# Whole-matrix Strassen products of a decoder layer: block sums on VectorE, additions by accumulating transfers

## The chip, the core and the metric

The kernel runs on one core of a Trainium2 chip. A core has a matmul engine (TensorE, here PE, with its weight load PEld), VectorE (DVE), ScalarE (ACT) and GpSimd (POOL), and SyncE (SP), which here issues all transfers. PE writes to PSUM, in banks of 128 x 512 fp32 numbers; the other operands lie in SBUF, 128 partitions wide. The metric is the device time of one execution in microseconds (us), median of the runs.

## The reference

One layer of a decoder trunk with x of 1024 tokens by 1024 features, fp32. Cut to what matters here:

```python
h  = rmsnorm(x)                      # three token mixers of h: A, B, C
m  = gate_a * A + gate_b * B + gate_c * C
x1 = x + m @ w_out                   # [1024,1024] @ [1024,1024]
h2 = rmsnorm(x1)
act = conv3(h2 @ w_up) * gelu(h2 @ w_gate)   # width 2816, schematic
x2 = x1 + act @ w_down               # [1024,2816] @ [2816,1024]
out = rmsnorm(x2)
```

## The kernel before

Activations lie feature-major, in tiles of 128 features by 1024 tokens. Each fp32 operand of a matmul is split into a high part (a cast on ACT, L96) and a low part (a subtraction, mostly on DVE, L97), and a product is made of three passes of a 128x128 weight against 512 columns. Instructions are put in order by a scheduler from the program's text; each engine then runs its own list in that order.

The end of the attention merges the three branches: `merge_c` makes the third branch's product tile by tile, DVE multiplies the bank by its gate (gc, L1131), and POOL adds the result onto the sum of the other two (ga, L1132). The second half of the tokens is done first. yc is the operand of these products.

`strassen_full` (L720) multiplies a whole matrix by Strassen's scheme in Winograd's form: weights and activations are cut into 2 x 2 blocks, there are seven products instead of eight, and their operands are sums of blocks. It is called for w_out (4 slices of the inner dimension) and for w_down (11 slices). Its items are (p, j): product p in the order 0, 1, 2, 3, 5, 4 and slice j. An item has 12 matmuls (4 output tiles by 3 passes), one of p = 2 has 24, since it stands for two products. For each item, one after the other and a little ahead of the matmuls: `loads` has SP fetch the weight blocks (fr) and activations (act), `sums` makes the block sums in place (S1 L785, T3 L786 and S2 L787 on POOL, T2 L788 and T1 L789 on DVE, all for p = 2; S3 L793, T4' L796 and S4 L800 on POOL for p = 3, 4 and 5), and `splits` makes fw (weights) and ft (activations). When a product has ended, `after(p)` says what is done with its PSUM banks: ACT copies a bank to a tile (cc, L834), SP loads the residual block x and an engine adds the copy (`add_x`, L824 and L825), later products are added from PSUM (`plus`, L829). What is put off by `later` is spread over the next items, three pieces at each.

A finished block goes to `done`. For w_out that is `done1`: the block's operands for the FFN (hb, T1 to T4), its store, and its square, which POOL adds to a running sum ssb, one sum for each half of the tokens (L952); a matmul of ssb with ones (L134), a root on ACT and a few steps on DVE (L119 to L127) give 1/rms (rs), which a matmul with ident (L142) spreads over the partitions. While the last sums come, PE makes F0, the first FFN weight tile's products, 96 matmuls with hb. For w_down `done2` squares by `add_sq` (L160), with the addition on DVE (L168). The FFN between the two, about 821 to 1234 us of the span, is made by pairs of weight tiles and is not touched.

Of the kernel before, what the change touches and what calls it, by code (L numbers as in the profile page):

```python
# [18 lines left out]
P = 128  # L19
# [10 lines left out]
# columns of the small packed constants  # L30
# [9 lines left out]
# columns of the wide packed constants  # L40
# [7 lines left out]
def trunk_kernel(  # L48
# [65 lines left out]
    def rsqrt(a, n, act=True):  # L114
        """a ** -0.5 on a positive [P, n] tile: an estimate (from a square root, or halved exponent bits), then
        Newton's steps."""
        y, t = tiny(n, "rs0", 2), tiny(n, "rs1", 2)
        if act:
            nc.scalar.activation(out=t, in_=a, func=AF.Sqrt)  # L119
            nc.vector.reciprocal(out=y, in_=t)  # L120
        else:
            nc.vector.tensor_scalar(out=y.bitcast(I32), in0=a.bitcast(I32), scalar1=-0.5, scalar2=float(0x5f3759df),
                                    op0=ALU.mult, op1=ALU.add)
        for _ in range(1 if act else 3):
            nc.vector.scalar_tensor_tensor(out=t, in0=y, scalar=-0.5, in1=y, op0=ALU.mult, op1=ALU.mult)
# [11 lines left out]
    def bcast_rows(rs, nt, dst, pool):  # L137
        """dst[:, t*128 + n] = rs[n, t] on all partitions."""
# [21 lines left out]
    def add_sq(acc, blk, alloc):  # L160
        """acc + blk ** 2, acc None at first."""
# [15 lines left out]
    def op2(src, alloc, n="op"):  # L177
        """two operands from a [P, 1024] tile."""
# [12 lines left out]
    # [feature, token] operands of a normalised activation, block by block  # L191
    class Act:
# [5 lines left out]
        def winograd(self, xt, j, T4=True, eng=None):  # L198
            """the block sums of slice j, made in place."""
# [15 lines left out]
        def block(self, kt, j):  # L215
            """name the operand of a block."""
# [3 lines left out]
    def prepare(src):  # L220
        """operands of a pair of weight tiles."""
# [25 lines left out]
    def strassen_pair(src, h, alloc_ps, mid=lambda: None):  # L247
        """both [128, 1024] products of a pair of weight tiles."""
# [59 lines left out]
    def scaled(kt, j):  # L308
        """operands of x times the gain; the token's factor follows the product."""
# [10 lines left out]
    def squares(kt, j):  # L320
        """sums of squares, in two parts."""
# [38 lines left out]
    # keeps the tensor engine's clock up until the first operands are there  # L360
# [15 lines left out]
    def rel_bias():  # L376
        """relative-position bias, one value per distance, replicated over 128 rows in DRAM."""
# [97 lines left out]
    # lambda of the differential attention, on all partitions  # L475
# [8 lines left out]
    # DRAM scratch  # L484
# [7 lines left out]
    # values of the attention, token-major  # L492
# [33 lines left out]
    def pooling(zb):  # L526
        """means over the trailing windows minus the value, feature-major."""
# [22 lines left out]
    def gating(f):  # L550
        """spatial gating (two groups at once; the diagonal blocks are kept)."""
# [42 lines left out]
    # q, k feature-major, stored as hi / lo  # L594
# [21 lines left out]
    def load_head(hd):  # L616
        """steps of the loads of a head."""
# [30 lines left out]
    def scores(t, c):  # L648
        """one map's exponentials of a query tile (the scores are negated)."""
# [40 lines left out]
    # the bias of zeros ties the table's load to the last gate  # L690
# [8 lines left out]
    def first_tiles():  # L699
        """the loads of the first head and its first scores."""  # L700
# [19 lines left out]
    def strassen_full(src, w, nsl, x_d, out, done, tail=None, LL=4):  # L720
        """steps of out[d][:, half] = (w.T @ src)[d tile] + x_d; w: [2*nsl, P, 1024], src(k): fp32 tile k, spent in
        place. done(d, half): what follows each block; tail(operands) takes over the last NL slices.
        The first LL steps only prepare."""
        pool, vec, sub, add = nc.gpsimd, nc.vector, ALU.subtract, ALU.add
        LS, LP = 2, 2
        SE = (nc.gpsimd, nc.gpsimd, nc.gpsimd, nc.vector, nc.vector, nc.gpsimd, nc.gpsimd, nc.gpsimd)
# [15 lines left out]
        def wh(p, k, lo_, c):  # L742
            """column half c of weight tile lo_ + k, two tiles at a time."""
# [36 lines left out]
        def sums(p, j):  # L780
            b11, b12, b21, b22 = blocks(j) if p > 1 else [None] * 4
            if p == 2:
                r, q, k = T[p, j]
                t1 = c2("T1")
                SE[0].tensor_tensor(out=q, in0=r[:, NH:], in1=q, op=add)          # S1  # L785
                SE[1].tensor_tensor(out=b12, in0=b22, in1=b12, op=sub)            # T3  # L786
                SE[2].tensor_tensor(out=k, in0=q, in1=r[:, :NH], op=sub)          # S2  # L787
                SE[3].tensor_tensor(out=b11, in0=b12, in1=b11, op=add)            # T2  # L788
                SE[4].tensor_tensor(out=t1, in0=b22, in1=b11, op=sub)             # T1  # L789
                T[p, j] = (k, b11), (q, t1)  # L790
            if p == 3:
                r = T[p, j]
                SE[5].tensor_tensor(out=r[:, :NH], in0=r[:, :NH], in1=r[:, NH:], op=sub)  # S3  # L793
                T[p, j] = (r[:, :NH], b12),
            if p == 4:
                SE[6].tensor_tensor(out=b21, in0=b21, in1=b11, op=sub)            # T4'  # L796
                T[p, j] = (T[p, j], b21),
            if p == 5:
                r = T[p, j]
                SE[7].tensor_tensor(out=r, in0=r, in1=keep(j), op=sub)            # S4  # L800
# [13 lines left out]
        B, X, C = {}, {}, {}  # L814
# [12 lines left out]
        def plus(d, j, other, eng):  # L827
            t = out(d, j)
            eng.tensor_tensor(out=t, in0=t, in1=other, op=ALU.add)  # L829

        def copy(key, d):
            if d % 2 == 0:
                C[key, d // 2] = a4([P, 2, NH], n="cc")
            nc.scalar.copy(C[key, d // 2][:, d % 2, :], B[0][d])  # L834

        def cc(key, d):
            return C[key, d // 2][:, d % 2, :]
# [5 lines left out]
        def after(p):  # L843
            R4 = range(4)
            if p == 0:
                for d in R4:
                    later(1, copy, 0, d)
                    later(1, lambda d: add_x(d, 0, cc(0, d), pool), d)
            if p == 1:
                for d in R4:  # L850
                    plus(d, 0, B[1][d], vec)
                for d in R4:
                    fin(d, 0, 3)
            if p == 2:
                for d in R4:
                    copy(2, d)
                for d in R4:
                    later(3, lambda d: add_x(4 + d, 1, B[2][d], vec), d)
                    later(4, lambda d: add_x(d, 1, cc(2, d), pool), d)
            if p == 3:  # L860
                for d in R4:
                    copy(3, d)
                for d in R4:
                    later(4, lambda d: plus(4 + d, 1, cc(3, d), pool), d)
                    fin(4 + d, 1, 5)
                for d in R4:
                    later(4, lambda d: add_x(4 + d, 0, cc(3, d), pool), d)
            if p == 5:
                for d in R4:
                    plus(d, 1, B[2][d], vec)  # L870
                    fin(d, 1, 5)
            if p == 4:
                for d in R4:
                    plus(4 + d, 0, B[4][d], vec)
# [6 lines left out]
        for n in range(-LL, len(items)):  # L881
            for st_ in stages:
                # operands of the held slices are made ahead
# [4 lines left out]
            if n >= 0:  # L888
# [18 lines left out]
                if p == 4 and tail:  # L907
                    if j == nsl - NL - 1:
                        for d in range(4):
                            plus(4 + d, 0, B[4][d], vec)  # L910
# [17 lines left out]
    def op_g(src, g, n):  # L928
        """operand of src times a gain."""
# [6 lines left out]
    def done1(d, j):  # L936
# [8 lines left out]
        def square():  # L945
# [22 lines left out]
        def t2():  # L968
            # T3 first: it needs the raw block
# [32 lines left out]
    def combine(t):  # L1002
        """rows scaled by sum0: P0 - (lam * sum0 / sum1) * P1."""
# [10 lines left out]
    def transpose(t, g):  # L1014
        """four key blocks of a query tile."""
# [13 lines left out]
    def attend(t):  # L1029
        """steps of the product with the values; tokens on the partitions."""  # L1030
# [16 lines left out]
    def sub_norm(hd, js, pool):  # L1047
        """rms norm over the head's channels; the rows carry the factor sum0."""
# [74 lines left out]
    def merge_c(banks):  # L1123
        for n_, (j, m) in enumerate((j, m) for j in (1, 0) for m in range(KT)):
# [7 lines left out]
            nc.gpsimd.tensor_tensor(out=mg[m][:, half(j)], in0=mg[m][:, half(j)], in1=gc, op=ALU.add)  # L1132
# [108 lines left out]
    # FFN down, final norm  # L1241
# [16 lines left out]
    def scale_out(k, j, sl, r, eng):  # L1258
        """two output blocks."""
# [28 lines left out]
    def tail2(hold):  # L1288
        """the last blocks, a quarter of the tokens at a time."""
# [94 lines left out]
def _layout(i):  # L1384
    """Layouts of the inputs, and constants of the shapes alone."""
# [10 lines left out]
    def pairs(wa, wb):  # L1396
        """[pair, (first, second), p, 8 * 128]: the second's K halves are swapped."""
# [65 lines left out]
```

## Time and profile before

| what | value |
|---|---|
| three runs | 1494.07, 1494.66, 1498.56 us; median 1494.66 |
| span of the profiled execution | 1492.7 us |
| busy PE, DVE, ACT, POOL | 1373.6, 1091.0, 649.0, 827.3 us |
| w_out (first matmul on ft, fw) to the first FFN pair | 671 to 821 us |
| w_down, without the tail | about 1235 to 1465 us |

The span is that of one execution under the profiler, without what lies around it, and is 2.0 us below the median of the runs. "PE busy" is no proof of PE at its peak: at full rate its matmuls overlap, so the number of matmuls that start in a window is the better measure. An arrow in a row points from the waiting engine to the one whose result it waited for.

### The profile page before, as it was taken

What the parts mean: (1) busy time and instruction counts of PE and PEld (TensorE: products, weight loads), DVE (VectorE), ACT (ScalarE), POOL (GpSimd) and SP (SyncE); (2) the same over time, 40 slices, a digit from 0 to 9 for tenths busy, and PEclk for the clock granted to TensorE, in tenths of its full rate; (3) what the DMA queues carried; (4) which work ended last, traced back from release to release, by engine and by line L of the source; (5) the groups of instructions that cost most, each with busy time, mean ns of one, the idle gap of its engine ahead of it and who ended that gap; (6) DMA issues with size and microseconds to landing.
All of it is one profiled execution on the core that took longest, in us unless ns stands there. A gap on an engine that the chain in (4) does not pass through costs nothing. (4 is left out here: it accounts for less than half of the span.)

```text
span 1492.7 us, 17887 instructions
## 1 busy us (share of the span) xinstructions
PE 1373.6 (92%) x6502; PEld 1137.8 (76%) x6502; DVE 1091.0 (73%) x1402; ACT 649.0 (43%) x1057; POOL 827.3 (55%) x499
## 2 busy tenths in 40 slices
PE   7899999999998989897875999999999999689887
PEld 6698778888886877786654888888888888478776
DVE  8764766444446899887899566877778789896783
ACT  7342234344445666523454434333333344154551
POOL 6423366555545454367597455666666624956724
PEclk9899999999999999998998999999999999899998
DMA  5232154333349954434521122222222268335413
GB/s 179 91 114 93 44 189 148 113 113 113 114 126 279 258 157 141 149 119 132 192 85 57 57 71 92 78 85 85 85 85 85 85 218 316 128 97 178 163 64 113
DMA packets 72496, 189.97 MB, mean 127 GB/s; under 512 B 7566, under 2 KB 16910, under 8 KB 72408
## 3 DMA queue, kind: packets, MB, share of 16 engines
q1 hardware_dynamic: 72408, 188.83, 38.2%
q8 instruction: 51, 0.84, 0.2%
q14 instruction: 37, 0.30, 0.1%
HBM read 143.70 MB, written 47.46 MB: 128 GB/s over the span
## 5 line engine op out<-in xcount | busy, mean ns | idle before, releaser
L185 PE MATMUL b<-ft,fw 128*128 128x512 f32 (+1 forms) x1308 | 307.2, 394 | 43.4 <-DVE fw L97 16.6
L185 PEld LDWEIGHTS b<-ft,fw 128*128 128x128 f32 x1308 | 245.8, 194 | 102.2 <-DVE fw L97 19.0
L347 POOL TENSOR_TENSOR F<-F,RB 128x1024 f32<-128x1024 f32 x74 | 190.5, 2575 | 164.6 <-DVE F L256 145.7
L256 DVE TENSOR_TENSOR F<-b,c 128x512 f32<-128x512 f32 x152 | 100.8, 683 | 125.8 <-ACT c L275 71.5
L185 PE MATMUL b<-hb,Ah 128*128 128x512 f32 x608 | 191.5, 395 | 0.0
L97 DVE TENSOR_TENSOR Sl<-s,Sh 128x1024 fp32r<-128x1024 f32 x76 | 150.8, 1985 | 42.6 <-PE b L185 23.5
L228 POOL TENSOR_TENSOR s<-r 128x512 f32<-128x512 f32 x38 | 60.8, 1599 | 194.5 <-DMA r<-in_w_up 77.4
L185 PE MATMUL b<-T,Sh 128*128 128x512 f32 x504 | 154.3, 389 | 0.0
L185 PEld LDWEIGHTS b<-hb,Ah 128*128 128x128 f32 x608 | 115.2, 190 | 25.1 <-issue 1.0
L185 PE MATMUL b<-hb,Al 128*128 128x512 f32 x304 | 119.5, 393 | 0.8 <-DVE Al L97 0.8
L96 ACT CAST Sh<-s 128x1024 fp32r<-128x1024 f32 x76 | 80.0, 1053 | 89.0 <-DVE Al L97 51.9
L97 DVE TENSOR_TENSOR Al<-r,Ah 128x1024 fp32r<-128x1024 f32 x38 | 77.5, 2038 | 50.8 <-ACT Ah L96 36.1
L185 PEld LDWEIGHTS b<-T,Sh 128*128 128x128 f32 x504 | 94.6, 188 | 19.8
L97 DVE TENSOR_TENSOR fw<-fr,fw 128x512 fp32r<-128x512 f32 x90 | 86.5, 976 | 19.7 <-ACT fw L96 18.6
L185 PE MATMUL b<-T,Sl 128*128 128x512 f32 x252 | 96.9, 389 | 0.0
L185 PE MATMUL b<-hb,Sh 128*128 128x512 f32 x304 | 94.1, 391 | 1.4 <-DVE F L256 1.4
L96 ACT CAST fw<-fr 128x512 fp32r<-128x512 f32 x90 | 54.3, 621 | 80.4 <-DVE fw L97 31.1
L96 ACT CAST Ah<-r 128x1024 fp32r<-128x1024 f32 x38 | 40.0, 1052 | 100.9 <-PE b L185 97.4
L185 PE MATMUL b<-Tl,Sh 128*128 128x512 f32 x204 | 79.4, 389 | 0.0
L185 PE MATMUL b<-Th,Sh 128*128 128x512 f32 x204 | 78.7, 390 | 0.7 <-ACT c L266 0.7
L185 PE MATMUL b<-Th,Sl 128*128 128x512 f32 x204 | 78.5, 389 | 0.0
L97 DVE TENSOR_TENSOR ft<-act,ft 128x512 fp32r<-128x512 f32 x66 | 73.5, 1141 | 4.8 <-ACT ft L96 4.8
(259 smaller groups left out, 3170.5 us busy)
## 6 DMA issues: line engine op xcount, KB each, us to landing
fr<-in_w_down SPq DMA_DIRECT2D x47, 512.0 KB, 3.8
r<-in_w_up SPq DMA_DIRECT2D x42, 512.0 KB, 3.7
r<-in_w_gate SPq DMA_DIRECT2D x24, 512.0 KB, 4.1
g_d<-F SPq DMA_DIRECT2D x24, 512.0 KB, 5.0
act_d<-cv SPq DMA_DIRECT2D x22, 512.0 KB, 2.6
act<-act_d SPq DMA_DIRECT2D x22, 512.0 KB, 6.3
fr<-in_w_out SPq DMA_DIRECT2D x18, 512.0 KB, 3.8
x<-in_xT SPq DMA_DIRECT2D x32, 256.0 KB, 5.1
```

The source lines that it names most:

```text
L96: nc.scalar.copy(hi, src)
L97: (eng or nc.vector).tensor_tensor(out=lo, in0=src, in1=hi.bitcast(F32), op=ALU.subtract)
L185: nc.tensor.matmul(ps, lhsT=w[a], rhs=x[b], start=first and i == 0, stop=last and i == 2, skip_group_check=more)
L228: nc.gpsimd.tensor_tensor(out=s1[:, :NH], in0=a21, in1=a22, op=ALU.add)
L256: nc.vector.tensor_tensor(out=o, in0=ps, in1=c, op=ALU.add)
L347: (eng or nc.gpsimd).tensor_tensor(out=F, in0=F, in1=RB, op=ALU.mult)
```

## The change

All eight block sums run on DVE. A new function `accumulate` has POOL issue a transfer that adds its source onto its destination in SBUF. It takes the place of three kinds of additions: the residual (`start`: ACT copies the bank into the output tile, then x is accumulated onto it from DRAM; the SP load, the cc tiles and `add_x` go), the squares' sums (in `done1`, then on POOL, and in `add_sq`, then on DVE), and the merge's last addition (POOL). There are 32, 14, 10 and 16 of them, 72 in all, each of 128 x 512 fp32 numbers, 256 KB. Comments are taken out too, which moves line numbers.

```diff
+    def accumulate(dst, src):
+        nc.gpsimd.dma_start(out=dst, in_=src, accum_op=ALU.add)
...
     def add_sq(acc, blk, alloc):
...
-        nc.vector.tensor_tensor(out=acc, in0=acc, in1=sq, op=ALU.add)
+        accumulate(acc, sq)
...
-                SE[0].tensor_tensor(out=q, in0=r[:, NH:], in1=q, op=add)          # S1
-                SE[1].tensor_tensor(out=b12, in0=b22, in1=b12, op=sub)            # T3
-                SE[2].tensor_tensor(out=k, in0=q, in1=r[:, :NH], op=sub)          # S2
+                vec.tensor_tensor(out=q, in0=r[:, NH:], in1=q, op=add)
+                vec.tensor_tensor(out=b12, in0=b22, in1=b12, op=sub)
+                vec.tensor_tensor(out=k, in0=q, in1=r[:, :NH], op=sub)
...
-        def add_x(d, j, other, eng):
+        def start(d, j, bank):
             t = out(d, j)
-            nc.sync.dma_start(out=t, in_=x_d[d, :, half(j)])
-            eng.tensor_tensor(out=t, in0=t, in1=other, op=ALU.add)
+            nc.scalar.copy(t, bank)
+            accumulate(t, x_d[d, :, half(j)])
...
             if p == 0:
                 for d in R4:
-                    later(1, copy, 0, d)
-                    later(1, lambda d: add_x(d, 0, cc(0, d), pool), d)
+                    later(1, start, d, 0, B[0][d])
...
             if p == 2:
                 for d in R4:
-                    copy(2, d)
+                    start(d, 1, B[0][d])
                 for d in R4:
-                    later(3, lambda d: add_x(4 + d, 1, B[2][d], vec), d)
-                    later(4, lambda d: add_x(d, 1, cc(2, d), pool), d)
+                    later(3, start, 4 + d, 1, B[2][d])
             if p == 3:
                 for d in R4:
-                    copy(3, d)
+                    start(4 + d, 0, B[0][d])
+                    later(4, plus, 4 + d, 1, B[0][d])
                 for d in R4:
-                    later(4, lambda d: plus(4 + d, 1, cc(3, d), pool), d)
                     fin(4 + d, 1, 5)
-                for d in R4:
-                    later(4, lambda d: add_x(4 + d, 0, cc(3, d), pool), d)
...
-                nc.gpsimd.tensor_tensor(out=stat[j], in0=stat[j], in1=sq, op=ALU.add)
+                accumulate(stat[j], sq)
...
-            nc.gpsimd.tensor_tensor(out=mg[m][:, half(j)], in0=mg[m][:, half(j)], in1=gc, op=ALU.add)
+            accumulate(mg[m][:, half(j)], gc)
```

The order of the instructions changes at three places. The first is POOL at the end of w_out, where the squares of both halves of the tokens are summed (two ssb, told apart by their last number) and the operands T2 and T3 are split (L97). Before:

```order
L952 TENSOR_TENSOR ssb_6482<-ssb_6482,sq_6644 128x512
L952 TENSOR_TENSOR ssb_6482<-ssb_6482,sq_6663 128x512
L952 TENSOR_TENSOR ssb_6482<-ssb_6482,sq_6707 128x512
L952 TENSOR_TENSOR ssb_6215<-ssb_6215,sq_6725 128x512
L952 TENSOR_TENSOR ssb_6482<-ssb_6482,sq_6718 128x512
L952 TENSOR_TENSOR ssb_6215<-ssb_6215,sq_6732 128x512
L97 TENSOR_TENSOR T_1373_6777<-x_555_3645,T_1373_6777 128x512
L952 TENSOR_TENSOR ssb_6215<-ssb_6215,sq_6739 128x512
L97 TENSOR_TENSOR T_1374_6786<-x_551_3641,T_1374_6786 128x512
L97 TENSOR_TENSOR T_1376_6801<-x_556_3646,T_1376_6801 128x512
L97 TENSOR_TENSOR T_1377_6804<-x_552_3642,T_1377_6804 128x512
L952 TENSOR_TENSOR ssb_6215<-ssb_6215,sq_6746 128x512
```

After:

```order
L104 DMA ssb_6494<-sq_6638 128x512
L104 DMA ssb_6209<-sq_6707 128x512
L104 DMA ssb_6494<-sq_6682 128x512
L104 DMA ssb_6209<-sq_6714 128x512
L104 DMA ssb_6494<-sq_6693 128x512
L104 DMA ssb_6209<-sq_6721 128x512
L97 TENSOR_TENSOR T_1367_6759<-x_555_3645,T_1367_6759 128x512
L97 TENSOR_TENSOR T_1368_6768<-x_551_3641,T_1368_6768 128x512
L97 TENSOR_TENSOR T_1370_6783<-x_556_3646,T_1370_6783 128x512
L97 TENSOR_TENSOR T_1371_6786<-x_552_3642,T_1371_6786 128x512
L104 DMA ssb_6494<-sq_6700 128x512
L104 DMA ssb_6209<-sq_6728 128x512
```

The additions have become transfers (DMA), the two sums take turns, and four T splits stand ahead of each sum's last addition.

The second is DVE in the merge, where it empties the banks (gc; `at`, `sc`, `mm` are PSUM tiles) and makes yc's low part. Before:

```order
L1131 TENSOR_TENSOR gc_5647<-at_5769,gc_5647 128x512
L932 SCALAR_TENSOR_TENSOR yc_5722<-ms_5717,cs,yc_5722 128x512
L1131 TENSOR_TENSOR gc_5740<-at_5784,gc_5740 128x512
L1131 TENSOR_TENSOR gc_5762<-mm_5799,gc_5762 128x512
L1131 TENSOR_TENSOR gc_5458<-mm_5814,gc_5458 128x512
L1131 TENSOR_TENSOR gc_5527<-sc_5829,gc_5527 128x512
L97 TENSOR_TENSOR fw_5978<-fr_5891,fw_5978 128x512
L1131 TENSOR_TENSOR gc_5584<-sc_5844,gc_5584 128x512
```

After:

```order
L1122 TENSOR_TENSOR gc_5647<-at_5769,gc_5647 128x512
L97 TENSOR_TENSOR fw_5956<-fr_5891,fw_5956 128x512
L789 TENSOR_TENSOR ga_3705<-ga_4558,ga_3705 128x512
L789 TENSOR_TENSOR ga_3846<-ga_4814,ga_3846 128x512
L923 SCALAR_TENSOR_TENSOR yc_5722<-ms_5717,cs,yc_5722 128x512
L1122 TENSOR_TENSOR gc_5740<-at_5784,gc_5740 128x512
L1122 TENSOR_TENSOR gc_5762<-mm_5799,gc_5762 128x512
L789 TENSOR_TENSOR ga_4066<-ga_5050,ga_4066 128x512
L1122 TENSOR_TENSOR gc_5458<-mm_5814,gc_5458 128x512
L1122 TENSOR_TENSOR gc_5527<-sc_5829,gc_5527 128x512
L97 TENSOR_TENSOR fw_5978<-fr_5891,fw_5978 128x512
L789 TENSOR_TENSOR ga_4322<-ga_5295,ga_4322 128x512
```

The sums T3 (L789, ga from ga and ga), which POOL made before, now stand among the evacuations, two of them ahead of yc's.

The third is PE in the last product of w_down, where the squares of one half of the tokens are summed over the partitions. Before, the product's banks being b_11338 to b_11341:

```order
L185 MATMUL b_11338<-ft_11311,fw_11308 128x512 x3
L185 MATMUL b_11339<-ft_11311,fw_11308 128x512 x3
L185 MATMUL b_11340<-ft_11311,fw_11308 128x512 x3
L185 MATMUL b_11341<-ft_11311,fw_11308 128x512 x3
L185 MATMUL b_11338<-ft_11317,fw_11314 128x512 x3
L185 MATMUL b_11339<-ft_11317,fw_11314 128x512
L134 MATMUL b_11408<-ones,ssb_11069 128x1 x4
L185 MATMUL b_11339<-ft_11317,fw_11314 128x512 x2
L185 MATMUL b_11340<-ft_11317,fw_11314 128x512 x3
```

After, the banks being b_11302 to b_11305:

```order
L189 MATMUL b_11302<-ft_11287,fw_11284 128x512 x3
L189 MATMUL b_11303<-ft_11287,fw_11284 128x512 x3
L189 MATMUL b_11304<-ft_11287,fw_11284 128x512 x3
L189 MATMUL b_11305<-ft_11287,fw_11284 128x512 x3
L189 MATMUL b_11302<-ft_11293,fw_11290 128x512 x3
L189 MATMUL b_11303<-ft_11293,fw_11290 128x512
L138 MATMUL b_11372<-ones,ssb_11065 128x1 x4
L189 MATMUL b_11303<-ft_11293,fw_11290 128x512 x2
L189 MATMUL b_11304<-ft_11293,fw_11290 128x512 x3
```

The matmul with ones stood behind 40 matmuls of the product, and now stands behind 64; POOL's list there has seven transfers onto ssb in a row, of which the last four belong to blocks that product 5 finishes.

## Rows read from the trace of the kernel before

**Rows 1.** Page, part 1: busy time, share, instructions of each engine.
```profile
PE 1373.6 (92%) x6502; PEld 1137.8 (76%) x6502; DVE 1091.0 (73%) x1402; ACT 649.0 (43%) x1057; POOL 827.3 (55%) x499
```

**Rows 2.** Windows: busy time and starts of each engine, clock, DMA share.
```profile
core 0: us, PE busy (x) PEld busy (x) DVE busy (x) ACT busy (x) POOL busy (x), PEclk, DMA share, GB/s
670.00:790.00 120.00, 96.73 (x393) 75.29 (x392) 104.70 (x93) 54.16 (x94) 89.96 (x57) 0.94 0.39 129
790.00:830.00 40.00, 23.96 (x101) 18.36 (x100) 32.73 (x31) 18.91 (x33) 28.56 (x17) 0.79 0.15 47
1240.00:1260.00 20.00, 20.00 (x90) 16.57 (x89) 19.30 (x22) 11.59 (x21) 10.28 (x7) 1.00 0.97 366
1260.00:1340.00 80.00, 61.98 (x251) 48.47 (x250) 73.23 (x67) 27.61 (x52) 61.59 (x38) 0.94 0.37 122
1340.00:1360.00 20.00, 20.00 (x90) 16.55 (x89) 8.98 (x13) 6.34 (x11) 8.00 (x6) 1.00 0.31 93
1380.00:1440.00 60.00, 54.34 (x229) 43.51 (x228) 49.48 (x53) 30.56 (x56) 36.85 (x23) 0.97 0.41 141
1440.00:1460.00 20.00, 15.91 (x65) 13.04 (x64) 8.93 (x18) 8.56 (x14) 0.00 (x0) 0.83 0.00 1
```

**Rows 3.** PE's waits, 671 to 821: total, times, longest (us).
```profile
PE b L142 <- DVE rs L127: 15.2, 1, 15.2
PE b L185 <- DVE x L829: 6.7, 2, 6.2
PE b L185 <- DVE ft L97: 6.3, 6, 1.9
PE b L185 <- ACT cc L834: 5.4, 1, 5.4
```

**Rows 4.** PE's waits, 1240 to 1480.
```profile
PE b L185 <- DVE fw L97: 16.6, 5, 8.2
...
PE b L134 <- DVE ssb L168: 4.1, 1, 4.1
```

**Rows 5.** Tile ga: DVE's splits, ns min/median/max, first and last start.
```profile
L97 DVE TENSOR_TENSOR ft<-ga,ft x24: 677/1751/1784, 661.7 to 771.2; 128x512 fp32r<-128x512 f32 x24
```

**Rows 6.** Timeline, two stretches: DVE alone, DVE beside POOL.
```profile
1433.22 4.29 DVE L97 TENSOR_TENSOR ft<-act,ft 128x512 fp32r<-128x512 f32 x7
...
698.45 1.70 POOL L825 TENSOR_TENSOR x<-x,cc 128x512 f32<-128x512 f32 x1
698.96 1.74 DVE L97 TENSOR_TENSOR ft<-T,ft 128x512 fp32r<-128x512 f32 x1
```

**Rows 7.** DMA view: transfers of 256 KB, median us from issue to landing.
```profile
x<-in_xT SPq DMA_DIRECT2D x32, 256.0 KB, 5.1
...
kh<-qk_d SPq DMA_DIRECT2D x16, 256.0 KB, 7.6
...
out<-x SPq DMA_DIRECT2D x8, 256.0 KB, 2.5
```

**Rows 8.** Lines: POOL's residual additions, busy us, mean ns, idle before.
```profile
L825 POOL TENSOR_TENSOR x<-x,cc 128x512 f32<-128x512 f32 x24 | 40.2, 1692 | 0.4 <-DMA x<-x_d 0.3
```

**Rows 9.** Timeline at 1271: ACT's wait for a load.
```profile
1271.04 0.62 ACT L96 CAST ft<-act 128x512 fp32r<-128x512 f32 x1 [7.04 <-DMA act<-act_d]
```

**Rows 10.** Timeline of the passage from w_out to the first FFN tile.
```profile
787.86 1.27 DVE L829 TENSOR_TENSOR x<-x,b 128x512 f32<-128x512 f32 x2
...
789.20 0.62 ACT L951 ACTIVATE sq<-x 128x512 f32<-128x512 f32 x1
...
804.08 5.08 DVE L978 SCALAR_TENSOR_TENSOR x<-x,cs 128x512 f32<-128x512 f32 x3
...
805.25 6.71 POOL L97 TENSOR_TENSOR T<-x,T 128x512 fp32r<-128x512 f32 x4
...
819.11 1.22 PE L142 MATMUL b<-ident,rs 128*128 128x128 f32 x4 [15.16 <-DVE rs L127]
```

**Rows 11.** Timeline at the merge: yc's low part, and its use.
```profile
649.86 0.75 DVE L932 SCALAR_TENSOR_TENSOR yc<-ms,cs,yc 128x512 fp32r<-128x512 f32 x1 [0.60 <-ACT yc L931]
...
655.11 0.61 PE L185 MATMUL mm<-yc,ph 128*128 128x512 f32 x2
```

More of the change, by code (lines that the diff above doesn't have):

```diff
@@ L720, in strassen_full @@
     def strassen_full(src, w, nsl, x_d, out, done, tail=None, LL=4):
-        pool, vec, sub, add = nc.gpsimd, nc.vector, ALU.subtract, ALU.add
+        vec, sub, add = nc.vector, ALU.subtract, ALU.add
         LS, LP = 2, 2
-        SE = (nc.gpsimd, nc.gpsimd, nc.gpsimd, nc.vector, nc.vector, nc.gpsimd, nc.gpsimd, nc.gpsimd)
         items = [(p, j) for p in (0, 1, 2, 3, 5, 4) for j in range(nsl)]
@@ L784, in sums @@
                 t1 = c2("T1")
-                SE[0].tensor_tensor(out=q, in0=r[:, NH:], in1=q, op=add)
-                SE[1].tensor_tensor(out=b12, in0=b22, in1=b12, op=sub)
-                SE[2].tensor_tensor(out=k, in0=q, in1=r[:, :NH], op=sub)
-                SE[3].tensor_tensor(out=b11, in0=b12, in1=b11, op=add)
-                SE[4].tensor_tensor(out=t1, in0=b22, in1=b11, op=sub)
+                vec.tensor_tensor(out=q, in0=r[:, NH:], in1=q, op=add)
+                vec.tensor_tensor(out=b12, in0=b22, in1=b12, op=sub)
+                vec.tensor_tensor(out=k, in0=q, in1=r[:, :NH], op=sub)
+                vec.tensor_tensor(out=b11, in0=b12, in1=b11, op=add)
+                vec.tensor_tensor(out=t1, in0=b22, in1=b11, op=sub)
                 T[p, j] = (k, b11), (q, t1)
@@ L792, in sums @@
                 r = T[p, j]
-                SE[5].tensor_tensor(out=r[:, :NH], in0=r[:, :NH], in1=r[:, NH:], op=sub)
+                vec.tensor_tensor(out=r[:, :NH], in0=r[:, :NH], in1=r[:, NH:], op=sub)
                 T[p, j] = (r[:, :NH], b12),
             if p == 4:
-                SE[6].tensor_tensor(out=b21, in0=b21, in1=b11, op=sub)
+                vec.tensor_tensor(out=b21, in0=b21, in1=b11, op=sub)
                 T[p, j] = (T[p, j], b21),
@@ L799, in sums @@
                 r = T[p, j]
-                SE[7].tensor_tensor(out=r, in0=r, in1=keep(j), op=sub)
+                vec.tensor_tensor(out=r, in0=r, in1=keep(j), op=sub)
                 T[p, j] = (r, b22),
@@ L812, in mm @@
                     first and j == 0, j == n - 1, more)
-        B, X, C = {}, {}, {}
+        B = {}
         bg = []
@@ L819, in later, with plus @@
             bg.append((due, f, a))
-        def add_x(d, j, other, eng):
+        def start(d, j, bank):
             t = out(d, j)
-            nc.sync.dma_start(out=t, in_=x_d[d, :, half(j)])
-            eng.tensor_tensor(out=t, in0=t, in1=other, op=ALU.add)
-        def plus(d, j, other, eng):
+            nc.scalar.copy(t, bank)
+            accumulate(t, x_d[d, :, half(j)])
+        def plus(d, j, bank):
             t = out(d, j)
[L829 to L837, printed above, removed]
+            vec.tensor_tensor(out=t, in0=t, in1=bank, op=ALU.add)
         def fin(d, j, due):
@@ L846, in after @@
                 for d in R4:
-                    later(1, copy, 0, d)
-                    later(1, lambda d: add_x(d, 0, cc(0, d), pool), d)
+                    later(1, start, d, 0, B[0][d])
             if p == 1:
                 for d in R4:
-                    plus(d, 0, B[1][d], vec)
+                    plus(d, 0, B[1][d])
                 for d in R4:
@@ L855, in after @@
                 for d in R4:
-                    copy(2, d)
+                    start(d, 1, B[0][d])
                 for d in R4:
-                    later(3, lambda d: add_x(4 + d, 1, B[2][d], vec), d)
-                    later(4, lambda d: add_x(d, 1, cc(2, d), pool), d)
+                    later(3, start, 4 + d, 1, B[2][d])
             if p == 3:
                 for d in R4:
-                    copy(3, d)
+                    start(4 + d, 0, B[0][d])
+                    later(4, plus, 4 + d, 1, B[0][d])
                 for d in R4:
-                    later(4, lambda d: plus(4 + d, 1, cc(3, d), pool), d)
                     fin(4 + d, 1, 5)
-                for d in R4:
-                    later(4, lambda d: add_x(4 + d, 0, cc(3, d), pool), d)
             if p == 5:
                 for d in R4:
-                    plus(d, 1, B[2][d], vec)
+                    plus(d, 1, B[2][d])
                     fin(d, 1, 5)
@@ L873, in after @@
                 for d in R4:
-                    plus(4 + d, 0, B[4][d], vec)
+                    plus(4 + d, 0, B[4][d])
                     fin(4 + d, 0, 6)
@@ L909, in strassen_full @@
                         for d in range(4):
-                            plus(4 + d, 0, B[4][d], vec)
+                            plus(4 + d, 0, B[4][d])
                 elif j == nsl - 1:
```

## The prediction

> **What bounds the kernel now.** I read the page's first part first: PE is busy for 92% of the span, DVE for 73%, POOL for 55% [rows 1]. The other 8% are some 119 us in which PE does nothing, and the question is which of them lie in the two places that the diff touches. The windows answer it [rows 2]. At full rate PE starts 90 matmuls of 512 columns in 20 us, 0.222 us each (1340 to 1360). Against that rate the whole-matrix product for w_out (670 to 790) starts 393 instead of 540 and loses 147 x 0.222 = 32.7 us; the passage from it to the first FFN tile (790 to 830) starts 101 instead of 180 and loses 17.5; the product for w_down loses 109 x 0.222 = 24.2 in 1260 to 1340, 41 x 0.222 = 9.1 in 1380 to 1440 and 25 x 0.222 = 5.6 in 1440 to 1460. Together 89 us. In the lossy windows DVE is near full (104.7 of 120, 73.2 of 80) and POOL busy too, and in 1340 to 1360, with POOL at 8 of 20, nothing is lost.
>
> The waits name the engine [rows 3, 4]: PE waits for DVE, once for 15.2 us on the root of the mean square (L127), else on splits (L97) and on PSUM additions (L829). Why DVE is late shows in its durations. The same subtraction of 128x512 with two SBUF inputs takes 677 ns at best and 1751 at the median for the operands out of the merge [rows 5]. Seven in a row, with POOL idle, go by in 4.29 us, 0.61 each from start to start; beside a POOL addition one takes 1.74, and the POOL addition 1.70 [rows 6]. So the two engines hold each other up, and the loss belongs to POOL's additions and sums in these stages.
>
> **The change part by part.** X stands below for the time from a POOL issue of an accumulating transfer of 256 KB to its landing. The trace has no transfer of POOL's. Its nearest rows are SP's transfers of the same size [rows 7]: 2.5 (a store), 5.1 (a load from the same tensor that the residuals come from), 7.6 (the slowest). Two of the slowest in a row, 15.2, is the upper bound, for a transfer that must fetch its destination as well. I take 5, the nearest row in what is read. What a page says of this stands apart: the Trainium skill, "DMA: Bandwidth & Descriptors", section "Anatomy of one DMA", has a transfer issued by GpSimd cost about 2.0 us and its bytes over 436 GB/s. By that X would be an estimated 2.6, and the sum below some 14 us lower, 1432; no run here shows it for an accumulating one.
>
> 1. POOL loses 90 block sums (S1, T3, S2, S3, T4' and S4 of 15 slices), 32 residual additions, 14 additions of squares and 16 of the merge: 152 operations at 1.69 us or a little less [rows 8], up to 257 us in which DVE's two-input operations took up to 1.74 instead of 0.68. DVE gains the 90 sums, 61 us at 0.68, and loses 10 additions of squares.
>
> 2. Is DVE then fast enough? In product 2 a slice needs 5 sums and 4 splits from DVE, 9 x 0.61 = 5.5 us, while PE's 24 matmuls take 24 x 0.222 = 5.3: a tie. In products 3 to 5 it is 3 x 0.61 = 1.8 against 2.7 for 12 matmuls, in 0 and 1 two splits. Before, product 2 gave DVE 6 operations, 10.4 us when all met POOL.
>
> 3. What w_out's 32.7 us become: the waits on x and ft (6.7 and 6.3) go. The copies of full banks stay on ACT, so I keep the whole wait on cc, 5.4 [rows 3], and 4.6 for the tie and for the lead-in. Kept 10, gained 22.7.
>
> 4. w_down, 1260 to 1340. The longest wait is 8.2 on fw, and it goes with the contention. But the loads stay, and ACT stood 7.0 us for act there [rows 9]. I keep 7 of 24.2: gained 17.2. In 1380 to 1440 I keep 5 of 9.1: gained 4.1.
>
> 5. The passage, 790 to 830. Before, PE waited 15.2 us for the root, whose DVE steps stood behind scalings of 1.7 us beside POOL's T splits [rows 10]. After, the additions of squares are a chain of transfers, each waiting for the last one, issued in POOL's order. From the end of product 4: PSUM addition and square 2.0 (787.86 to 789.82 [rows 10]), two alternating steps 2X, four T splits on POOL at 1.68 (6.7, the row of four [rows 10], since DVE is busy beside them), the last accumulate X: 8.7 + 3X = 23.7. The matmul on ssb now stands 5 before the end of F0's 96, at 91 x 0.222 = 20.2. So PE waits 3.5, then 1.5 for the root, and 1.5 goes to the clock, which the passage shows at a mean of 0.79 now [rows 2]. Kept 6.5, gained 11.0. A second floor lies close below: some 25 DVE operations from product 4's end to the root, at 0.7 each and four of them slow, are 20 to 22 us too, so a smaller X gains at most 3 here.
>
> 6. The end of w_down. Seven squares are one chain, four of them after product 5: 3 + 4X = 23 from that product's end. PE reaches its ssb matmul after 64 matmuls, 14.2 us, and waits 8.8, with 2 for the clock; before it waited 4.1 [rows 4] and the window lost 5.6. Lost 5.2 more.
>
> 7. The merge. DVE now has the T3 sums between the evacuations of gc, each behind an accumulate. The second T3 stands right before yc's low part, which DVE gave out at 649.86 before and PE used at 655.11 [rows 11]. That leaves 5.2 us of cover, about X; then two more such waits pile up before the first ft. At X = 5 I count 1.
>
> The loads of x that SP no longer issues and the tiles that the copies no longer take I cost at nothing: no wait of PE's on either is among the rows. The accumulates into x cost nothing either while X is below 10: they are issued at a product's start, and the PSUM addition onto them comes at its end, 48 matmuls or 10.7 us later.
>
> Sum: -22.7 - 17.2 - 4.1 - 11.0 + 5.2 + 1 = -48.8 us. The profiled span of 1492.7 becomes 1443.9; the median of the runs, 1494.66, lies 2.0 above the span, so 1446.
>
> **The rivals.** (a) The chain decides. Above 5, each us of X costs 3 in the passage, 4 at the end and about 2 in the merge, 9 in all; the 48.8 are used up at X = 10.4, and at 15.2 the time is 1446 + 92 = 1538. For it: the chains are serial and POOL stands still in each wait, with T splits and later issues behind it. Against it: no row of 256 KB above 7.6. At 7.6 the time is 1469. The Trainium skill, same page, "Rules for kernel authors", says that an accumulate reads its destination and writes it later and that the next access must wait for its semaphore; so nothing would let the chain overlap, and no run before shows it. Chance that it takes the whole gain or more: 0.11.
>
> (b) DVE becomes the bound in product 2. If its operations don't overlap at 0.61 but follow at their 0.68, a slice takes 6.1 against 5.3, 0.8 x 15 = 12 us: 1458. For it: a tie leaves no room for additions from PSUM between. Against it: the row of seven. Chance 0.18. (That DVE's slowness isn't POOL's doing, so that 9 operations at 1.74 make 15.7 us a slice in product 2 and 156 us more over 15 slices, would end near 1600; the paired rows [rows 6] speak against it, 0.02.)
>
> (c) The loads bound w_down: DMA share 0.97 at 1240 to 1260 [rows 2] and ACT's wait for act. Then 20 of the 24.2 stay instead of 7: 1459. Against it: the share falls to 0.37 just where the loss is. Chance 0.12.
>
> **How the numbers follow.** The forecast, 1446, has 0.57. Low end: X = 2.5 takes away the end's wait (10.8), 3 in the passage and 1 in the merge, 1431, and half of the 22 kept in steps 3 and 4 gives 1420. High end: X = 7.6 together with (b) is 1481; I take 1480. Within 0.3% (4.5 us), about what a measurement can tell, is 0.03; slower, from (a) beyond 10.4 and the remark in (b), 0.11; the rest faster, 0.86.
>
> **What would show it.** Right: POOL's rows of 1.7 gone from both stages, DVE's fw and ft near 0.69, PE at 85 or more per 20 us in 1260 to 1340, the wait for rs below 5, one of 5 to 12 on ssb near the end, X read as issue to landing near 5. Wrong: waits on ssb, ga or x that add up to 49 (a), DVE full in product 2 with PE at 80 per 20 us (b), ACT waiting for act (c).

## The result, and the profile after

| | before | after |
|---|---|---|
| median of four runs, us | 1494.37 (1493.38 to 1498.56) | 1445.78 (1444.86 to 1449.65) |
| ratio, 95% interval | | 0.9676 (0.9660 to 0.9691) |
| forecast | | 1446, range 1420 to 1480 |
| span of the profiled execution | 1492.7 | 1448.0 |

The change is faster by 48.6 us, 3.2%. The profiled execution of after is the longest of its four (1449.65), so the trace below accounts for 44.7 of these. One of the four executions of e2, below, took 2262.21 us at a granted clock of 0.555 and is left out of its numbers. The first view to read is the timeline at the places where PE passes from one stage to the next. Of after:

```profile
672.23 1.07 PE L189 MATMUL b<-ft,fw 128*128 128x512 f32 x4
...
805.34 1.20 PE L189 MATMUL b<-hb,Ah 128*128 128x512 f32 x2
...
1203.60 0.62 PE L189 MATMUL b<-ft,fw 128*128 128x512 f32 x2
...
1420.77 0.39 PE L1290 MATMUL b<-ones,ssb 128*128 128x1 f32 x3
```

and the same four starts in the trace of before:

```profile
671.20 0.62 PE L185 MATMUL b<-ft,fw 128*128 128x512 f32 x2
...
820.83 0.77 PE L185 MATMUL b<-hb,Ah 128*128 128x512 f32 x1
...
1218.83 0.39 PE L185 MATMUL b<-ft,fw 128*128 128x512 f32 x1
...
1465.60 0.28 PE L1299 MATMUL b<-ones,ssb 128*128 128x1 f32 x2
```

Their differences are the stages (w_down begins at 1218.8, earlier than the 1235 given ahead, and its last product runs on into the tail):

| stage, us | before | after | difference | forecast |
|---|---|---|---|---|
| up to w_out | 671.2 | 672.2 | +1.0 | +1 |
| w_out and the passage to the FFN | 149.6 | 133.1 | -16.5 | -33.7 |
| FFN pairs | 398.0 | 398.3 | +0.3 | 0 |
| w_down | 246.8 | 217.2 | -29.6 | -16.1 |
| tail | 27.1 | 27.2 | +0.1 | 0 |

So the sum came out and two of its parts did not: w_out gave 17 us less than forecast, w_down 13 more. The windows of after show the same. The columns are those of [rows 2]:

```profile
672.00:762.00 90.00, 80.69 (x338) 65.19 (x337) 71.09 (x96) 52.58 (x93) 33.17 (x34) 0.94 0.81 198
762.00:806.00 44.00, 27.52 (x116) 22.44 (x115) 31.48 (x41) 20.27 (x34) 22.48 (x20) 0.77 0.43 96
1215.00:1280.00 65.00, 65.00 (x289) 53.83 (x288) 64.01 (x103) 34.36 (x62) 4.41 (x5) 1.00 0.81 269
1280.00:1320.00 40.00, 36.73 (x148) 29.53 (x147) 28.68 (x48) 15.44 (x28) 1.73 (x2) 0.91 0.40 114
1320.00:1400.00 80.00, 77.83 (x342) 63.58 (x341) 60.39 (x98) 49.35 (x92) 14.01 (x16) 1.00 0.71 189
1400.00:1420.00 20.00, 20.00 (x100) 16.71 (x99) 3.69 (x10) 4.39 (x8) 2.59 (x3) 1.00 0.28 49
```

At 90 matmuls per 20 us, w_down's 1280 to 1400 lacks 50 matmuls, 11 us, where before lost 39 from 1260 to 1460 [rows 2]. From 1215 to 1280 DVE is busy for 64.0 of 65 us and PE misses nothing; PE is in products 0 and 1 there, until 1269, and DVE makes product 2's sums and splits ahead of it. The first window, w_out's 336 matmuls, lacks 67, 14.9 us. The second is the passage with F0: 96 matmuls, 21.3 us of work, in 43.2. The page's first part gives DVE 80 operations more than before and less busy time, 1013.6 us against 1091.0 [rows 1]:

```profile
PE 1364.5 (94%) x6502; PEld 1137.7 (79%) x6502; DVE 1013.6 (70%) x1482; ACT 651.7 (45%) x1065; POOL 644.4 (45%) x419
```

The groups by line, busy and mean, show why: DVE's splits take about their time alone, against the 1.75 us of [rows 5]:

```profile
L97 DVE TENSOR_TENSOR fw<-fr,fw 128x512 fp32r<-128x512 f32 x90 | 62.3, 710 | 6.6 <-ACT fw L96 5.6
L97 DVE TENSOR_TENSOR ft<-act,ft 128x512 fp32r<-128x512 f32 x66 | 44.0, 695 | 3.4 <-ACT ft L96 3.4
L97 DVE TENSOR_TENSOR ft<-ga,ft 128x512 fp32r<-128x512 f32 x24 | 16.2, 687 | 5.4 <-ACT ft L96 5.3
```

PE's waits from 600 to 820, and behind the dots from 1180 to 1440 (answers to [rows 3] and [rows 4]; the wait on ssb at the end of w_down is gone):

```profile
PE b L138 <- DMA ssb<-sq: 8.4, 1, 8.4
PE b L146 <- DVE rs L131: 8.0, 1, 8.0
PE b L189 <- DVE ft L97: 5.6, 1, 5.6
...
PE b L189 <- DVE fw L97: 3.6, 2, 2.6
```

And the transfers, in the view of [rows 7]:

```profile
ssb<-sq POOLq DMA_DIRECT2D x24, 256.0 KB, 4.2
...
ga<-gc POOLq DMA_DIRECT2D x16, 256.0 KB, 5.3
...
x<-in_xT POOLq DMA_DIRECT2D x16, 256.0 KB, 8.1
...
x<-x_d POOLq DMA_DIRECT2D x16, 256.0 KB, 8.5
```

X, taken as 5, is 4.2 and 5.3 in the median where a chain or the next reader waits for it, and 8.1 to 8.5 for the residuals, issued up to eight in a row and not on the path.

### The profile page after: what moved, and what is told of

Same layout as the page of the kernel before. It is cut to its first block, busy times and chain, and to the rows that moved or that the text cites. A ratio compares the mean times of both kernels' runs of the same rounds, so it can differ in the third digit from the quotient of the medians.

```text
span 1448.0 us, 17868 instructions
## 1 busy us (share of the span) xinstructions
PE 1364.5 (94%) x6502; PEld 1137.7 (79%) x6502; DVE 1013.6 (70%) x1482; ACT 651.7 (45%) x1065; POOL 644.4 (45%) x419
## 5 line engine op out<-in xcount | busy, mean ns | idle before, releaser
L189 PE MATMUL b<-ft,fw 128*128 128x512 f32 (+1 forms) x1308 | 298.0, 388 | 14.8 <-DVE ft L97 6.8
L189 PEld LDWEIGHTS b<-ft,fw 128*128 128x128 f32 x1308 | 243.3, 191 | 66.8 <-DVE ft L97 8.3
L97 DVE TENSOR_TENSOR Sl<-s,Sh 128x1024 fp32r<-128x1024 f32 x76 | 149.3, 1964 | 42.7 <-PE b L189 24.0
L97 DVE TENSOR_TENSOR Al<-r,Ah 128x1024 fp32r<-128x1024 f32 x38 | 77.0, 2026 | 53.1 <-ACT Ah L96 38.2
L104 POOL DMA_DIRECT2D ssb<-sq x24 | 21.1, 906 | 117.9 <-ACT sq L171 38.2
L189 PE MATMUL b<-wh,hb 128*128 128x256 f32 x384 | 71.8, 286 | 0.0
```

What stands on the lines that cost most here:

```text
L97: (eng or nc.vector).tensor_tensor(out=lo, in0=src, in1=hi.bitcast(F32), op=ALU.subtract)
L104: nc.gpsimd.dma_start(out=dst, in_=src, accum_op=ALU.add)
L189: nc.tensor.matmul(ps, lhsT=w[a], rhs=x[b], start=first and i == 0, stop=last and i == 2, skip_group_check=more)
```

## The experiments

Each is timed in rounds with the kernel before on one chip, and the ratio to it is what is compared; after has 0.9676 (0.9660 to 0.9691).

### The parts alone: the sums, the transfers

Edit of the kernel before, e1:

```diff
-        SE = (nc.gpsimd, nc.gpsimd, nc.gpsimd, nc.vector, nc.vector, nc.gpsimd, nc.gpsimd, nc.gpsimd)
+        SE = (nc.vector,) * 8
```

> The kernel before with all eight block sums on DVE; residuals, squares and the merge's addition stay where they were. If POOL's two-input operations beside DVE are what costs (contention), 90 of POOL's 152 go and most of the gain comes: 1458 to 1472 us, with DVE's fw and ft means near 0.75 us and only stretches beside the residual additions slow. If it is POOL's list that is late, with the sums as harmless fillers, DVE gets 61 us more to do and the time stays above 1485.

Edit of after, e2 (one of six lines, S1, T3, S2, S3, T4', S4):

```diff
-                vec.tensor_tensor(out=q, in0=r[:, NH:], in1=q, op=add)
+                nc.gpsimd.tensor_tensor(out=q, in0=r[:, NH:], in1=q, op=add)
```

> The changed kernel with the sums S1, T3, S2, S3, T4' and S4 back on POOL, so that the accumulating transfers stand alone. Contention: 90 POOL operations stay beside DVE's splits, the time lies at 1470 to 1482 us and DVE's splits in product 2 still show 1.7 us. If the residuals and squares on POOL's list were the delay, most of the gain stays: below 1458.

Measured: e1 1458.38 us, 0.9751 (0.9733 to 0.9770), 36.5 won; e2 1479.27 us (median of three), 0.9889 (0.9865 to 0.9912), 15.6 won. Together that is 52.2 against 48.6, by the ratios 0.0360 against 0.0324: the parts add up to the whole or, at the edge of the intervals, to a little more. In e1 the mean of DVE's splits is 839 ns (fw) and 758 (ft of act), where near 750 was expected; before it was 976 and 1141. In e2 DVE has 90 operations fewer than in after and PE still waits 11.6 us for fw from 1195 to 1475; its groups by line:

```profile
L97 DVE TENSOR_TENSOR fw<-fr,fw 128x512 fp32r<-128x512 f32 x90 | 88.1, 993 | 26.1 <-ACT fw L96 25.1
L97 DVE TENSOR_TENSOR ft<-act,ft 128x512 fp32r<-128x512 f32 x66 | 66.1, 1036 | 4.9 <-ACT ft L96 4.9
```

With less to do DVE is slower at it, 993 and 1036 ns against 710 and 695, beside POOL's sums.

These two runs don't separate two things that a sum on POOL does: it slows DVE, and it comes late itself, at 1.5 to 1.7 us each in a row on POOL's list. In w_down of before, ACT waited 30.9 us for POOL's weight sums; the largest part, six waits from 1218 to 1466, was for S2:

```profile
ACT fw L96 <- POOL S L787: 21.4, 6, 7.6
```

The runs e4 and e4b below put work beside DVE without moving a sum.

### The residual and the merge

e6 puts the functions `add_x`, `copy`, `cc` and `after` of the kernel before back into after; e7 puts back the merge's line:

```diff
-            accumulate(mg[m][:, half(j)], gc)
+            nc.gpsimd.tensor_tensor(out=mg[m][:, half(j)], in0=mg[m][:, half(j)], in1=gc, op=ALU.add)
```

> The changed kernel with the residuals as before: SP loads x, ACT copies banks to cc tiles, POOL makes 24 of the additions and DVE 8; sums on DVE and squares and merge by transfers stay. The sums alone won 36 of the 49 us; if the rest belongs to the residual additions (24 of POOL's remaining operations, right beside DVE's splits), this run gives back 9 to 14: 1454 to 1460. If it belongs to squares or merge, it stays within 3 of the changed kernel, 1443 to 1449.

> The changed kernel with the merge's last addition on POOL again. By the prediction the transfers there cost about 1 us and win nothing, so 1443 to 1447. If POOL's 16 additions beside DVE's evacuations cost more than the transfers' landings, 1449 to 1453.

Measured: e6 1455.72 us, 0.9739 (0.9725 to 0.9754), 0.0063 above after or 9.4 us; e7 1445.79 us, 0.9674 (0.9659 to 0.9688), no difference. The residual by transfers is worth 9 us, together with what comes with it (eight `plus` additions go from POOL to DVE, the cc tiles and the loads by SP go), in w_down 223.0 instead of 217.2 and in w_out with the passage 137.9 instead of 133.1. The merge's win nothing and cost nothing that is measured.

### POOL's presence by itself

e4 and e4b leave all of after's work as it is and add POOL additions of 128x128 behind each moved sum of w_down, four in e4 and two in e4b, whose results nothing uses:

```diff
+    def dummy(n, t):
+        for i in range(4 if n > 4 else 0):          # e4b: 2
+            u = t[:, i * P:(i + 1) * P]
+            nc.gpsimd.tensor_tensor(out=dm, in0=u, in1=u, op=ALU.add)
...
                 vec.tensor_tensor(out=q, in0=r[:, NH:], in1=q, op=add)
+                dummy(nsl, q)
```

> The changed kernel with additional POOL additions in w_down that nothing uses: four of 128x128 after each of the 66 sums that moved, reading the sum and writing a scratch tile, so that DVE's work, the transfers and every result stay as they are. Contention: DVE's two-input operations slow down again and w_down loses 8 to 25 us, 1454 to 1470. If POOL's presence costs nothing by itself, within 2 us of the changed kernel.

> Half as many unused POOL additions as in the run before (two of 128x128 after each moved sum of w_down, 132 in all, some 1.3 us a sum, near what the sums took on POOL before). If what the first run lost came from contention alone, about half of its 44 us stays: 1460 to 1472. If it came from POOL's list running late, so that the tiles its additions read come free late, it falls away once POOL keeps up: 1446 to 1456.

Measured: e4 1489.72 us, 0.9967 (0.9946 to 0.9988), 44 lost against after; e4b 1464.81 us, 0.9801 (0.9774 to 0.9828), 19 lost. By the starts as above, w_down takes 251.2 and 237.0 us instead of 217.2; w_out with the passage stays at 133.4 and 133.0. So POOL work whose results nothing uses takes back two thirds of what w_down won (e4b), or all of it (e4; before had 246.8). e4 lost more than I expected of contention alone. Groups by line of e4b, 1200 to 1420:

```profile
L119 POOL TENSOR_TENSOR dm<-fr 128x128 f32<-128x128 f32 x66 | 66.7, 1011 | 31.9 <-DVE fr L806 13.9 <-DVE fr L795 11.1 <-DVE fr L815 2.4
...
L97 DVE TENSOR_TENSOR ft<-act,ft 128x512 fp32r<-128x512 f32 x64 | 47.1, 763 | 0.6 <-ACT ft L96 0.6
```

DVE's split rises from 684 ns (after, same stretch) to 763, so a part is contention. But the added work also reads the tiles and stands ahead of the transfers on POOL's list (PE waits 1.9 us on ssb in e4b and 4.9 in e4). How much belongs to which isn't separated by these two runs.

### The passage: chain, splits or DVE

e3 puts w_out's additions of squares on DVE; e9 puts the T2 and T3 splits on DVE; e8 does both:

```diff
-                accumulate(stat[j], sq)
+                nc.vector.tensor_tensor(out=stat[j], in0=stat[j], in1=sq, op=ALU.add)
...
-            hh.T[i]["T2"] = op1(b[3], "T2", nc.gpsimd)
+            hh.T[i]["T2"] = op1(b[3], "T2")
...
-            hh.T[i]["T3"] = op1(b[1], "T3", nc.gpsimd)
+            hh.T[i]["T3"] = op1(b[1], "T3")
```

> The changed kernel with the 14 additions of squares at the end of w_out on DVE instead of accumulating transfers. If the chain of transfers makes PE wait at the end of F0 (8.4 us on ssb, and the start of the root after it), the time falls by 5 to 12 us, 1434 to 1441, and the wait on ssb is gone. If DVE's own lateness there is the cause (an operation of 9.1 us at 748 and the scalings behind it), it stays within 2 us of the changed kernel, and 14 more operations can even cost 1 to 3.

> The changed kernel with the splits T2 and T3 at the end of w_out on DVE instead of POOL; the chain of transfers onto ssb stays. If POOL's T splits are what holds the root (they stand between the chain's steps, and ACT's copies and casts wait for them), PE's two waits at the end of F0 (8.4 and 8.0 us) shrink to under 6 together and the time falls by 8 to 13 us, 1433 to 1438. If the transfers' own landing sets the end, the wait on ssb stays above 6 and no more than 4 us are won. If DVE's list is the bound there, its 8 more operations cost and the time is 1446 to 1452.

> The T2 and T3 splits on DVE and the 14 additions of squares on DVE too, so that POOL has nothing to do in that passage but the T1 sums and the weight sums of the FFN. If splits and chain each hold the root alone (taking the chain away alone won 2.9), both together win 10 to 16 us: 1430 to 1436. If DVE is the bound, it wins no more than the squares alone, 1441 to 1446.

Measured: e3 1442.89 us, 0.9650 (0.9634 to 0.9667), 4 us better than after by the ratios, with intervals that just overlap; e9 1443.91 us, 0.9670 (0.9634 to 0.9706), not told from after; e8 1436.87 us, 0.9621 (0.9599 to 0.9643), 8 us better than after. PE's longest wait from 665 to 830, at the end of F0, in e3:

```profile
PE b L146 <- DVE rs L131: 17.3, 1, 17.3
```

and in e8:

```profile
PE b L146 <- DVE rs L131: 15.0, 1, 15.0
```

Without the chain PE waits as long as with it (8.4 + 8.0), now for the root alone. The expectation that the chain costs 5 to 12 us missed: it hides a second limit of the same length. With e8 that limit is still there, and DVE is the engine that is late. Rows of PE and DVE in e8 (F0's first matmul, the sum over the partitions, DVE's reading of it, the FFN's first matmul):

```profile
749.86 0.61 PE L189 MATMUL b<-hb,wh 128*128 128x512 f32 x2
...
768.99 0.94 PE L138 MATMUL b<-ones,ssb 128*128 128x1 f32 x8
...
786.48 0.15 DVE L158 TENSOR_SCALAR ssum<-b 128x4 f32<-128x4 f32 x1
...
794.34 1.20 PE L189 MATMUL b<-hb,Ah 128*128 128x512 f32 x2
```

DVE takes the sum up 16.6 us after it is done, without a pause in between: scalings, T splits and FFN weights stand ahead of it on its list. So what e3 and e8 win does not lie in the passage. From F0's first matmul to the FFN's they take 48.0 and 44.5 us, and after 43.2. It lies in w_out, 80.8 and 80.1 us where after takes 89.9: DVE's operation of 9.07 us (last section) and PE's wait of 5.6 us behind it are gone.

### The chain alone

e10 is the kernel before with only the edit of e3 in reverse: the 14 additions of squares at the end of w_out are transfers, everything else is as before.

> The kernel before with only the 14 additions of squares at the end of w_out as accumulating transfers. Alone they take 23 us off POOL where DVE is slow, but put the chain in: 1486 to 1497 us, with a wait on ssb near F0's end or the wait on the root as before. In four runs with such transfers single DVE operations of 128x512 took 5 to 9 us beside a run of POOL operations, and none over 2.4 without. If the transfers bring these, some appear between 700 and 815 here; if they come from POOL's list running free of sums and residuals, none does.

Measured: 1492.04 us, 0.9992 (0.9977 to 1.0007): no change that is clear of the interval. PE's one wait of 15.2 on the root [rows 3] becomes 11.5 on ssb and 7.5 on the root. And the slow DVE operations appear with the transfers: 3.42 and 3.40 us at 756 and 768, and 7.50 in the passage, where the trace of before has none of 128x512 above 2.4 from 630 to 820.

### w_down's squares, and the best version

e5 puts `add_sq`'s addition on DVE as before the change; e11 is e8 with e5:

```diff
-        accumulate(acc, sq)
+        nc.vector.tensor_tensor(out=acc, in0=acc, in1=sq, op=ALU.add)
```

> The changed kernel with the 10 additions of squares in w_down on DVE as before the change. In the trace of the changed kernel PE does not wait on ssb there, the last transfer landing just as PE comes to it, so the time should stay within 2 us of the changed kernel, 1444 to 1448. By the prediction's own term (a wait of 8.8 us) it would fall to 1435 to 1440.

> The candidate for the best: the changed kernel with all additions of squares (14 and 10) and the T2 and T3 splits on DVE. The two runs that changed one half each were at 0.9621 and 0.9649 of the kernel before, against 0.9676 for the change; if they add, 0.959 to 0.962, 1432 to 1437 us. If DVE is full there, no better than 0.9621.

Measured: e5 1440.85 us, 0.9649 (0.9626 to 0.9672), 4 us better than after by the ratios, with intervals that overlap; e11 1435.13 us, 0.9603 (0.9589 to 0.9617), clear of after. e11 differs from e9 in the additions of squares alone, all 24 of them, and is 10 us better by the ratios, clear of the intervals; its distance to e8, w_down's ten alone, is within them. w_down takes 211.0 us in e5 and 210.0 in e11, and 213.2 to 217.2 in after, e3, e7, e8 and e9, which have the transfers there. The chain at its end was no wait, so I expected nothing of e5, and was wrong about where it costs. DVE's waits in after, 1240 to 1330:

```profile
DVE T L792 <- DMA ssb<-sq: 6.2, 2, 5.4
DVE fr L796 <- DMA fr<-in_w_down: 3.8, 3, 1.6
```

The first row is T1's, which takes its tile from the pool of six that also holds sq. A square is held until its transfer has landed; T1 waits for that, and DVE, in order, with it, and PE's wait of 2.6 on fw at 1298 follows. In after PE takes 66.8 us for product 2's 264 matmuls, 1268.9 to 1335.7, and 60.0 in e5 and in e11; at 0.222 each they are 58.7. In e5 and e11 that row of DVE's is gone, and PE's waits on fw from 1180 to 1440 are 1.0 and 0.8 us, against 3.6.

## Why the prediction was right, and where it wasn't

**The mechanism** (steps 1 and 2) held in the main. POOL's two-input work beside DVE was the loss: e1 and e2 show the two halves, e4 and e4b that work which nobody needs costs too. How much of it was DVE's slowness, and how much POOL's sums that came late themselves (ACT's 30.9 us), stays open; the prediction named only the first. The Trainium skill, "SBUF — State Buffer", section "Who interferes with whom", has it that a DVE instruction with two SBUF inputs contends with a GpSimd instruction that reads SBUF; the trace agrees, 0.68 us alone [rows 5] and 1.74 beside [rows 6]. The tie in product 2 held as well: with the wait on ssb gone, in e5 and e11, PE loses 1.3 us in the whole of it, so rival (b) did not come. After alone would not tell it, since there product 2 loses 8.1 us with DVE not full (28.7 of 40 us from 1280 to 1320). Nor did (c).

**The chain's price**, X = 5, was near: 4.2 in the median, 3.8 from issue to issue at the end of w_down. By the fit of the Trainium skill, "DMA: Bandwidth & Descriptors", section "Anatomy of one DMA", a transfer of 256 KB would be an estimated 2.6; the trace disagrees for these, since that is lower than the shortest of the 24 onto ssb, 3.3. The residuals took up to 13.5, more than the 10 up to which the prediction let them cost nothing, but no wait of PE's is on one.

**Step 3**, kept 10, measured 14.9. The wait on full banks, kept at 5.4, was 1.7. The largest wait is 5.6 us for an ft that was late behind one DVE operation of 9.07 us (last section), and the 11 matmuls after it took 0.41 us each instead of 0.22, at a granted clock of 0.56 from 757.7 to 762: that is a cost which no step had.

**Step 4** kept 12 and measured 11.1, but its size came out for another reason than the one given. It kept 7 for the loads, and 7.1 are lost from 1280 to 1320; there the wait is on fw, behind DVE's T1 that waited for a transfer onto ssb, and in e5 and e11 product 2 is 6.8 us shorter without it. The tiles that the transfers hold were costed at nothing.

**Step 5** failed, kept 6.5 and measured 43.2 - 21.3 = 21.9. Three of its terms were mis-sized. The first is "PSUM addition and square 2.0". Rows of PE, DVE and ACT:

```profile
762.11 0.62 PE L189 MATMUL b<-hb,wh 128*128 128x512 f32 x2
...
772.24 0.68 DVE L832 TENSOR_TENSOR x<-x,b 128x512 f32<-128x512 f32 x1
...
773.58 0.62 ACT L942 ACTIVATE sq<-x 128x512 f32<-128x512 f32 x1
...
792.95 5.97 DVE L97 TENSOR_TENSOR T<-x,T 128x512 fp32r<-128x512 f32 x1 [9.68 <-ACT T L96]
```

F0 begins at 762.11 when product 4's matmuls end, and that product's last PSUM addition starts at 772.24, its square at 773.58: 12.1 us to the square's end, not 2.0. DVE was behind by a whole list: the operation of 9.07 us, then FFN weights and scalings that stand ahead of these additions. Chain and T splits then took 17.2 us, less than the 21.7 forecast (four splits took 6.03, the last square had landed by 791.4), and PE waited 8.4 for 3.5. The second is the root, 8.0 for 1.5, since DVE's T4 split ahead of it waited 9.7 for ACT, whose list waited for POOL's T splits (4.8, 1.9 and 3.6), and then took 5.97 itself. The third is the 1.5 for the clock: 5.5 us are left for it and for the small matmuls with ones and ident, which the sum had at nothing, and the granted clock was 0.50, the level of 1.2 GHz, from 791.4 to 806, behind the first wait. e3 and e8 show that neither the chain nor these splits alone is the bound: take both away and PE still waits 15.0 for DVE's list. The "second floor" of 20 to 22 us was named, but counted from product 4's end with an empty DVE. Steps 3 and 5 miss by 4.9 and 15.4, which is 20.3, and the stages by 17.2: counted by the stages, the kernel before lost 53.6 us there (149.6 less 432 matmuls at 0.222) and not the 50.2 of the prediction's two windows.

**Step 6** failed the other way: a wait of 8.8 was forecast and none came. The timeline at the end of product 5, the rows of PSUM addition, transfers and matmul:

```profile
1396.45 0.69 DVE L832 TENSOR_TENSOR x<-x,b 128x512 f32<-128x512 f32 x1 [0.95 <-PE b L189]
...
1398.10 0.86 POOL L104 DMA_DIRECT2D ssb<-sq  x1 [5.03 <-ACT sq L171]
...
1401.89 0.86 POOL L104 DMA_DIRECT2D ssb<-sq  x1 [2.93 <-ACT x L1254]
...
1405.66 0.86 POOL L104 DMA_DIRECT2D ssb<-sq  x1 [2.91 <-issue]
...
1409.48 0.86 POOL L104 DMA_DIRECT2D ssb<-sq  x1 [2.96 <-issue]
...
1412.91 1.02 PE L138 MATMUL b<-ones,ssb 128*128 128x1 f32 x8
```

A chain of 1.7 + 4 x 3.8 instead of 3 + 4 x 5; and it starts before the product has ended, since the first bank is done 9 matmuls before the fourth. PE comes to ones,ssb as the last transfer lands. That is worth 10.8 us of w_down's surplus of 13.5.

**Step 7**, +1, can't be told. w_out's first matmul starts 1.0 us later than before, but in the eight traces whose code is the same up to there it starts anywhere from 668.7 to 672.2, and e7 shows no difference.

Of the signs that the prediction named, three failed: PE starts 324 matmuls from 1260 to 1340, 81 and not 85 per 20 us, the wait for rs is 8.0 and not below 5, and there is none on ssb near the end.

So that the total came out within 1 us is luck: one error of -17 and one of +13.5 nearly met. The forecast of the whole deserves less trust than its closeness suggests; what the runs confirm is where the gain lies, 36.5 us in the sums (e1) and 9.4 in the residuals (e6).

## What to carry to other kernels

Where two engines slow each other, count each operation at its price beside the other engine, and read from a stretch where one rests what it costs alone; moving all of it to one engine can win even if that engine gets more to do (here its busy time fell). A transfer that adds is slower than the addition it replaces (4 to 5 us for 0.7), so it paid where nothing waits for it (the residual), and not for the squares, where it held tiles that another engine needed and came with held DVE operations. When a wait is moved off one path, ask what the waiting engine's list looks like at that moment, not only how long the new chain is.

## What was not expected of the hardware

Single DVE operations of 128x512 took 5 to 9 us in a run of POOL operations. The timeline of after, POOL and DVE and the matmul that waited:

```profile
747.23 0.87 POOL L104 DMA_DIRECT2D ssb<-sq  x1 [9.51 <-ACT ft L96]
...
747.79 1.63 POOL L956 TENSOR_TENSOR x<-x 128x512 f32<-128x512 f32 x1
747.98 9.07 DVE L97 TENSOR_TENSOR hb<-x,hb 128x512 fp32r<-128x512 f32 x1
...
749.06 1.62 POOL L232 TENSOR_TENSOR s<-r 128x512 f32<-128x512 f32 x1
...
750.31 1.62 POOL L234 TENSOR_TENSOR s<-r,r 128x512 f32<-128x512 f32 x1
...
753.99 1.21 POOL L104 DMA_DIRECT2D ssb<-sq  x1
754.60 1.89 POOL L233 TENSOR_TENSOR s<-s,r 128x512 f32<-128x512 f32 x1
...
757.71 4.56 PE L189 MATMUL b<-ft,fw 128*128 128x512 f32 x11 [5.59 <-DVE ft L97]
```

In [rows 6] and [rows 10] the two engines take turns, each at 1.7 us. Here POOL goes on at 1.25 us from start to start, near the 1.29 that such an operation of its takes with DVE idle, and DVE's one operation lasts until POOL's run ends. It came again at the same place, 8.0 to 8.9 us, in e4, e4b, e5 and e7, and in the passage at 5.97 or 5.98 in these; with other lists at 5.4 and 8.3 in e2, 7.5 in e6 and in e10. In e1, e3, e8, e9 and e11 there is none above 2.4 from 630 to 820, though e9 keeps the transfers onto ssb. e10 shows that the transfers, put among POOL's operations, bring it (up to 7.50 us) to a kernel that had none; whether by themselves or by the order of the lists that comes with them isn't shown. Why the turns stop, and what an operation must meet to be held, these runs leave open.
